# VectorE's seven-product work interleaved across row pairs, and more row pairs in that form, in a two-layer decoder trunk

## The chip, the cores and the metric

The kernel runs on one core of one Trainium2 chip. The metric is the device time of one execution in microseconds, from three runs given as a median with the lowest and the highest. TensorE (PE) multiplies, VectorE (DVE), ScalarE (ACT) and GpSimd (POOL) compute elementwise, and SyncE (SP) issues most of the weight transfers; each works through its own list of instructions in order and waits on semaphores for the others.

## What is computed

The reference is a trunk of two pre-norm layers on 256 tokens of width 2048, all in float32. Each layer has a token mixer beside a cross-attention into 256 memory tokens, an output projection, and a SwiGLU FFN of inner width 5632:

```python
for layer in range(DEPTH):                       # 2
    hn = _rmsnorm(h, norm_mix[layer])
    y, xq = _hgrn2_mixer(...) if layer == 0 else _gla_mixer(...)
    xa = _memory_attention(xq, mem_n, w_mem_kv[layer])
    h = h + jnp.concatenate([y, xa], axis=-1) @ w_out[layer]
    hn = _rmsnorm(h, norm_ffn[layer])
    gate, up = jnp.split(hn @ w_gate_up[layer], 2, axis=-1)
    h = h + (jax.nn.silu(gate) * up) @ w_down[layer]
return _rmsnorm(h, norm_final)
```

The two FFNs hold most of the work: a 2048 by 11264 product (gate and up together) and a 5632 by 2048 product each.

## The kernel before

**Float32 from three fast products.** A float32 factor is cut into a high part in the faster float32r type and a low part, the difference. One product of two tiles is three matmuls into one PSUM bank: high by high, high by low, low by high. For the weights `split` does the cutting (L276): ACT writes the high part (a CAST, or an ACTIVATE where the sign is turned), then DVE subtracts it from the raw weight and writes the low part (a TENSOR_TENSOR or SCALAR_TENSOR_TENSOR of 512 or 1024 columns). Twice in a block of the FFN POOL does the subtraction in DVE's place (`free_port`).

**Row pairs.** Weights come in row pairs: two blocks of 128 rows (the inner dimension), each with 512 columns of one kind (gate) and 512 of another (up), so that `raw` holds four 128x512 pieces. With the two token tiles of the activations this is a 2 by 2 product of blocks, and a pair has one of these kinds:

- **S**: seven products instead of eight (`seven`, L451), 21 matmuls. DVE must also form sums of weight pieces: `raw[:, 0]` becomes a difference (512 columns, called "less" here), then `raw[:, 2:4]` has it subtracted (1024 columns, "both less"). Four splits, named a (512 columns, of `raw[:, 0]`), b, c and d (1024 columns each): a and b before the sums, c and d of the sums. In the FFN the sum that c needs is put together by the transfer itself (`fed`): SP loads one row block into `raw[:, 1]`, then POOL issues an accumulating DMA of the other on top of it. For pairs 0 and 7 that sum lies in a tile of its own, T (`load_apart`).
- **O** and **H**: eight products, 24 matmuls. O needs two splits of 1024 columns on DVE and nothing else; H needs the same two, one difference of 512 columns and one split of 512 more. They use different sums of the activations, and `PAIRS` fixes for each pair which sums of activations are kept (`Forms`).
- In `project_two` (mixers, memory keys, output projection) the kinds are S and "-", a plain pair with eight products.

**The FFN.** `ffn` runs 11 blocks of 512 gate and 512 up columns (`up_block`). `project_halves` goes through the eight row pairs of a block with the kinds of `KINDS` (L1197): the fifth and later blocks all use its last entry, seven blocks in each layer. After each block come two "down" units of `project`, which multiply earlier results with `w_down` and accumulate onto `h` (`fd` in the trace); in the steady blocks these are four weight loads of 1024 KB. `sums` and `gate` turn the seven banks of a block (`f_p`) into the gated result, `turn` transposes it.

**What sets the order.** In the FFN the kernel's own order holds on each engine (`Engine.kept`). Small pieces of work (sums, gate, turn, `give_back`) are put off with `due` and come up at `mark(key + p)`, which `seven` calls between its splits b and c. `give_back` is two ACT copies of a down unit's PSUM banks to `h`; the steady blocks do it for their second unit inside pair 1 of the next block, ahead of split c of that pair. Buffers: `raw` has 3, `parts` (the 1024 column splits) 6, `part` (split a) 2; the pool waits for the last reader of a buffer before it is loaded or written again.

In the trace and in the order of the instructions the steady block that is looked at has the weight tiles 136 to 143 for row pairs 0 to 7 and 144 to 147 for its down units; `parts138c` is split c of pair 2, and `raw<-raw` are the two sums. The helper at L151 records nearly every operation of PE, DVE and ACT, so lines of code tell little there and tile names tell more.

## Time and profile before

| | |
|---|---|
| three runs | 2255.65 us median, 2253.49 to 2257.12 |
| the profiled execution | 2254.6 us, span of the core's instructions 2252.8 us |
| ACT busy | 1452.8 us, 64% of the span, 2010 instructions |
| POOL busy | 280.4 us, 12%, 275 instructions |
| PE weight loads busy | 1894.6 us, 84% (they overlap the matmuls) |
| mean granted TensorE clock | 0.999 of full speed |
| transfers | 477.28 MB, mean 212 GB/s |

Busy time is time in which an instruction of that engine ran; matmuls are pipelined and their ends are modelled, so that a busy PE tells that it was fed, and the spacing of its starts tells how fast. A timeline row has the start, the duration, the engine, the line, the operation, what is written and read, how many instructions were merged, and in brackets how long the engine stood idle before it and whose end it waited for. The fifth to eleventh blocks of an FFN are the steady ones: the fifth begins at 729.83 us in layer 0 and at 1773.06 us in layer 1, and the next ones follow every 61.45 to 61.69 us.

### The profile page before, as it was taken

What the parts mean: (1) busy time and instruction counts of PE and PEld (TensorE: products, weight loads), DVE (VectorE), ACT (ScalarE), POOL (GpSimd) and SP (SyncE); (2) the same over time, 40 slices, a digit from 0 to 9 for tenths busy, and PEclk for the clock granted to TensorE, in tenths of its full rate; (3) what the DMA queues carried; (4) which work ended last, traced back from release to release, by engine and by line L of the source; (5) the groups of instructions that cost most, each with busy time, mean ns of one, the idle gap of its engine ahead of it and who ended that gap; (6) DMA issues with size and microseconds to landing.
All of it is one profiled execution on the core that took longest, in us unless ns stands there. A gap on an engine that the chain in (4) does not pass through costs nothing.

```text
span 2252.8 us, 30400 instructions
## 1 busy us (share of the span) xinstructions
PE 2238.6 (99%) x10668; PEld 1894.6 (84%) x10668; DVE 2031.5 (90%) x2551; ACT 1452.8 (64%) x2010; POOL 280.4 (12%) x275
## 2 busy tenths in 40 slices
PE   9999999999999999999999999999999999999998
PEld 7888888888888888888889999988888888888887
DVE  6879899898998999999996887889999999999997
ACT  7656656565666666666665665566566676666664
POOL 1000100000111112112210000000011221212110
PEclk9999999999999999999999999999999999999999
DMA  8656655656687778878865445566677878887874
GB/s 296 215 168 213 199 182 177 200 193 190 198 236 232 229 234 231 230 230 238 244 221 168 141 156 182 164 209 197 208 221 224 233 230 238 242 238 236 231 233 167
DMA packets 255628, 477.28 MB, mean 212 GB/s; under 512 B 18255, under 2 KB 47731, under 8 KB 255219
## 3 DMA queue, kind: packets, MB, share of 16 engines
q1 hardware_dynamic: 228547, 420.21, 55.5%
q0 software_dynamic: 25632, 50.87, 13.0%
q10 hardware_dynamic: 1296, 4.26, 0.5%
q8 instruction: 84, 1.38, 0.2%
q14 instruction: 69, 0.57, 0.1%
HBM read 472.12 MB, written 3.15 MB: 211 GB/s over the span
## 4 chain that ended last, share of the span: by engine, by line
PE 90%; DVE 6%; issue 2%; DMA 1%; ACT 1%; SPq 0%; POOL 0%; DVEq 0%; POOLq 0%; ACTq 0%
PE f_p L151 34%; PE fd L151 18%; PE wo L151 4%; PE m1p L151 2%; PE hv2p L151 2%; PE hv1p L151 2%; PE hf0p L151 2%; PE hv0p L151 2%; PE wo1p L151 2%; PE hf2p L151 2%; PE hf1p L151 2%; PE wo0p L151 2%; PE m0p L151 2%; PE gk0p L151 1%; PE gk1p L151 1%
## 5 line engine op out<-in xcount | busy, mean ns | idle before, releaser
L151 DVE TENSOR_TENSOR raw<-raw 128x1024 f32<-128x1024 f32 (+3 forms) x330 | 311.2, 943 | 16.7 <-DMA raw<-in_w_down_dram 5.6
L151 ACT CAST parts<-raw 128x1024 fp32r<-128x1024 f32 (+1 forms) x216 | 211.7, 1016 | 56.8 <-DMA raw<-in_w_down_dram 14.7
L151 DVE TENSOR_TENSOR parts<-raw,parts 128x1024 fp32r<-128x1024 f32 (+1 forms) x176 | 200.2, 1171 | 22.7 <-ACT parts L151 22.0
L444 POOL DMA_DIRECT2D raw<-in_w_gate_up_dram x92 | 80.4, 873 | 541.2 <-DMA raw<-in_w_gate_up_dram 274.7
L300 POOL TENSOR_TENSOR parts<-raw,parts 128x1024 fp32r<-128x1024 f32 x40 | 95.6, 2406 | 113.5 <-ACT parts L151 81.2
L151 ACT COPY h<-fd 128x512 f32<-128x512 f32 x80 | 45.7, 588 | 46.5 <-PE fd L151 44.0
L428 POOL DMA_DIRECT2D T<-in_w_gate_up_dram x36 | 21.1, 587 | 430.2 <-DVE hf_4g L151 82.7
L151 ACT ACTIVATE s<-s,rf_r 128x512 f32<-128x512 f32 x44 | 31.8, 723 | 42.0 <-DVE s L151 42.0
L151 DVE SCALAR_TENSOR_TENSOR s<-e,rf_r,s 128x512 f32<-128x512 f32 x44 | 45.7, 1076 | 2.9 <-ACT s L151 0.5
L151 DVE TENSOR_TENSOR e<-f_p,e 128x512 f32<-128x512 f32 x66 | 45.2, 684 | 2.6 <-DVE s L151 0.5
L429 POOL DMA_DIRECT2D T<-in_w_gate_up_dram x36 | 31.0, 861 | 120.4 <-DMA T<-in_w_gate_up_dram 111.1
L151 ACT COPY fd<-h 128x512 f32<-128x512 f32 x82 | 45.2, 582 | 0.0
L444 POOL DMA_DIRECT2D raw<-in_hgrn_w_in_dram x17 | 14.7, 867 | 209.9 <-DMA raw<-in_hgrn_w_in_dram 124.6
L151 PE MATMUL fd<-parts,s_0h 128*128 128x512 f32 x128 | 39.8, 392 | 0.0
L151 PE MATMUL fd<-parts,s_4h 128*128 128x512 f32 x128 | 39.8, 392 | 0.0
L151 PE MATMUL fd<-parts,s_8h 128*128 128x512 f32 x128 | 39.8, 392 | 0.0
L151 PE MATMUL fd<-parts,s_2h 128*128 128x512 f32 x128 | 39.8, 392 | 0.0
L151 PE MATMUL fd<-parts,s_6h 128*128 128x512 f32 x128 | 39.8, 392 | 0.0
L151 PE MATMUL fd<-parts,s_1h 128*128 128x512 f32 x128 | 39.4, 389 | 0.0
L151 PE MATMUL fd<-parts,s_3h 128*128 128x512 f32 x128 | 39.4, 389 | 0.0
L151 PE MATMUL fd<-parts,s_5h 128*128 128x512 f32 x128 | 39.4, 389 | 0.0
L151 PE MATMUL fd<-parts,s_7h 128*128 128x512 f32 x128 | 39.4, 389 | 0.0
(6020 smaller groups left out, 7434.0 us busy)
## 6 DMA issues: line engine op xcount, KB each, us to landing
raw<-in_w_gate_up_dram SPq DMA_DIRECT2D x224, 512.0 KB, 4.4
raw<-in_w_down_dram SPq DMA_DIRECT2D x80, 1024.0 KB, 5.5
raw<-in_w_gate_up_dram SPq DMA_DIRECT2D x220, 256.0 KB, 4.2
raw<-in_hgrn_w_in_dram SPq DMA_DIRECT2D x79, 512.0 KB, 4.6
raw<-in_gla_w_in_dram SPq DMA_DIRECT2D x96, 384.0 KB, 3.3
raw<-in_w_gate_up_dram POOLq DMA_DIRECT2D x92, 256.0 KB, 4.9
T<-in_w_gate_up_dram POOLq DMA_DIRECT2D x72, 256.0 KB, 5.0
raw<-in_w_out_dram SPq DMA_DIRECT2D x16, 1024.0 KB, 5.1
```

The lines of the kernel that those rows point to most:

```text
L151: ins = func(*args, **kwargs)
L300: low = (nc.gpsimd if free_port else ve).tensor_tensor(out=both[:, 1, k:j, 0:m], in0=src[:, k:j, :], in1=both[:, 0, k:j, 0:m].bitcast(F32) ...
L428: nc.gpsimd.dma_start(out=both[:, 0, :], in_=rows[0])
L429: nc.gpsimd.dma_start(out=both[:, 0, :], in_=rows[1], accum_op=ALU.add)
L444: nc.gpsimd.dma_start(out=raw[:, 1, 0:n], in_=rows[1], accum_op=ALU.add)
```

## The change

Three things are changed.

1. **Interleaving.** `seven` gets an `ahead` call between its splits c and d: the tile of the next pair is taken, its loads are issued and its split a is done there, before split d of the present pair. "less" of a pair moves ahead of its split b, and "both less" comes after split b. With T apart, "both less" stands between the two halves of split c. In H pairs `ahead` comes before the small third split. `project_two` does the same where an S pair follows an S pair.
2. **More S pairs.** Row pair 5 keeps the activation sums of S (eight of them) in place of those of O (six). The fifth and later blocks of the FFN become `SSSSSSSS`, in the first four O becomes H at pair 5 (eight products as before). In the GLA mixer's key/query stages (`gk0`, `gk1`) there are two S pairs, not one.
3. **The order of the seven sums** of a block's banks in `sums`, and with it the two additions after which POOL takes a split.

```diff
-    def split(src, name, by=2, turned=False):
+    def split(src, name, by=2, turned=False, between=None):
...
+                if k:
+                    between()
...
-    PAIRS = "SSSSSOSB"
+    PAIRS = "SSSSSSSB"
...
-    def seven(i, raw, fed, between=None):
+    def seven(i, raw, fed, between=None, b00=None, ahead=None):
...
+        if not begun:
+            b00, = split(raw[:, 0:1, :], f"{i}a")
+        if not fed:
+            tt(out=raw[:, 1, :], in0=raw[:, 1, :], in1=raw[:, 2, :], op=ALU.add)
+        if fed and begun:
+            less()
         b11, b10 = split(raw[:, 2:4, :], f"{i}b")
         if between:
             between()
...
+        if not (fed and begun):
+            less()
+        if apart:
+            t6, t7 = split([raw[:, 0:1, :], apart], f"{i}c", turned=True, between=both_less)
+        else:
+            both_less()
+            t6, t7 = split(raw[:, 0:2, :], f"{i}c", turned=True)
+        if ahead:
+            ahead()
         t5, t4 = split(raw[:, 2:4, :], f"{i}d")
...
+        def ahead(p):
+            if p < len(PAIRS):
+                i, raw = come(p)
+                came.append((i, raw, split(raw[:, 0:1 if kinds[p] == "S" else 2, :], f"{i}a")))
...
-        project_two(hq["pairs"], ("------S-", "------S-")[pr], w, kw + pr * 2 * DK, pr * 2 * DK, 2 * DK, f"gk{pr}", give,
+        project_two(hq["pairs"], "-----SS-", w, kw + pr * 2 * DK, pr * 2 * DK, 2 * DK, f"gk{pr}", give,
...
-    KINDS = ("SHHSHOSO", "HHHSSOSO", "SHHSSOSO", "SSHSSOHS", "SSSSSOSS")
+    KINDS = ("SHHSHHSO", "HHHSSHSO", "SHHSSHSO", "SSHSSHHS", "SSSSSSSS")
...
-                for out, p, q in ((s0, 2, e0), (e1, 6, e0), (s1, 7, e1), (e1, 5, e1), (e0, 5, s1),
+                for out, p, q in ((e1, 6, e0), (s0, 2, e0), (s1, 7, e1), (e0, 5, s1), (e1, 5, e1),
                                   (s1, 4, s1), (e1, 3, e1)):
                     ve.tensor_tensor(out=out, in0=ps[p], in1=q, op=ALU.add)
-                    if p in (2, 5) and out is not e0 and b:
+                    if (p == 6 or out is e0) and b:
```

On DVE, in a steady block of layer 0, pair 2 (tile 138) and the start of pair 3 (139) stood so before; `raw_6651` is the tile of pair 2:

```order
L151 TENSOR_TENSOR parts138a<-raw_6651,parts138a 128x512
L151 TENSOR_TENSOR parts138b<-raw_6651,parts138b 128x1024
L151 TENSOR_TENSOR raw_6651<-raw_6651 128x512
L151 TENSOR_TENSOR raw_6651<-raw_6651 128x1024
L151 SCALAR_TENSOR_TENSOR parts138c<-raw_6651,parts138c 128x1024
L151 TENSOR_TENSOR parts138d<-raw_6651,parts138d 128x1024
L151 TENSOR_TENSOR parts139a<-raw_6691,parts139a 128x512
```

The same place on DVE now, from split a of pair 2 on; `raw_6652` is the tile of pair 2:

```order
L151 TENSOR_TENSOR parts138a<-raw_6652,parts138a 128x512
L151 TENSOR_TENSOR parts137d<-raw_6599,parts137d 128x1024
L151 TENSOR_TENSOR raw_6652<-raw_6652 128x512
L151 TENSOR_TENSOR parts138b<-raw_6652,parts138b 128x1024
L151 TENSOR_TENSOR raw_6652<-raw_6652 128x1024
L151 SCALAR_TENSOR_TENSOR parts138c<-raw_6652,parts138c 128x1024
L151 TENSOR_TENSOR parts139a<-raw_6692,parts139a 128x512
L151 TENSOR_TENSOR parts138d<-raw_6652,parts138d 128x1024
```

The six instructions of a pair are the same; split a of the next pair stands ahead of split d, and split b stands between the two sums, right ahead of the one that overwrites what it reads.

On DVE at pair 5 (tile 141), which was an O pair, and its neighbours, before:

```order
L151 TENSOR_TENSOR parts140d<-raw_6731,parts140d 128x1024
L151 TENSOR_TENSOR parts141a<-raw_6774,parts141a 128x1024
L151 TENSOR_TENSOR parts141b<-raw_6774,parts141b 128x1024
L151 TENSOR_TENSOR parts142a<-raw_6807,parts142a 128x512
L151 TENSOR_TENSOR parts142b<-raw_6807,parts142b 128x1024
```

The same place on DVE now:

```order
L151 TENSOR_TENSOR parts141a<-raw_6775,parts141a 128x512
L151 TENSOR_TENSOR parts140d<-raw_6732,parts140d 128x1024
L151 TENSOR_TENSOR raw_6775<-raw_6775 128x512
L151 TENSOR_TENSOR parts141b<-raw_6775,parts141b 128x1024
L151 TENSOR_TENSOR raw_6775<-raw_6775 128x1024
L151 SCALAR_TENSOR_TENSOR parts141c<-raw_6775,parts141c 128x1024
L151 TENSOR_TENSOR parts142a<-raw_6815,parts142a 128x512
L151 TENSOR_TENSOR parts141d<-raw_6775,parts141d 128x1024
```

Pair 5 has six instructions on DVE where it had two.

On ACT, at the start of that block, now; `h<-fd` are the two copies of `give_back`, `s_4h` belongs to `turn`:

```order
L151 CAST parts137b<-raw_6599 128x1024
L151 ACTIVATE s_4h<-tp_s_4h_6547 128x512
L151 ACTIVATE s_4h<-tp_s_4h_6552 128x512
L151 COPY h<-fd_1_3_0_0_6501 128x512
L151 COPY h<-fd_1_3_0_1_6502 128x512
L151 ACTIVATE parts137c<-raw_6599 128x1024
L151 CAST parts138a<-raw_6652 128x512
L151 CAST parts137d<-raw_6599 128x1024
```

Before, the first six of these rows stood in the same order; behind split c of pair 1 the cast of 137d came ahead of that of 138a, and now the two have changed places.

More of the change, by code (lines that the diff above doesn't have):

```diff
@@ L591, in early, with come @@
                 out[:] = onto
-        for at, (p, kind) in enumerate(zip(order, plan)):
+        came = []
+        def come(at):
             i, raw = new_raw()
             if i == 0:
-                load_pair(raw, w, p, c0, c1, n, kind, fed)
+                load_pair(raw, w, order[at], c0, c1, n, plan[at], fed)
             if prep:
@@ L599, in project_two, with ahead @@
             if i > 0:
-                load_pair(raw, w, p, c0, c1, n, kind, fed)
+                load_pair(raw, w, order[at], c0, c1, n, plan[at], fed)
+            return i, raw
+        def ahead(at):
+            i, raw = come(at)
+            came.append((i, raw, split(raw[:, 0:1, 0:n], f"{i}a")[0]))
+        for at, (p, kind) in enumerate(zip(order, plan)):
+            i, raw, b00 = came.pop() if came else (*come(at), None)
             if kind == "S":
-                todo = held(behind, seven, i, raw[:, :, 0:n], fed) if behind else seven(i, raw[:, :, 0:n], fed)
+                more = (lambda: ahead(at + 1)) if plan[at + 1:at + 2] == "S" else None
+                args = seven, i, raw[:, :, 0:n], fed, None, b00, more
+                todo = held(behind, *args) if behind else args[0](*args[1:])
                 last = at == plan.rindex("S")
@@ L638, in product, with come @@
             pe.matmul(ps[b], xl, hi, start=False, stop=left[b] == 0)
-        for p, kind in enumerate(kinds):
-            Engine.kept = keep <= p
+        came = []
+        def come(p):
             i, raw = new_raw()
@@ L644, in project_halves @@
                 apart[7] = load_apart(w, 7, c1)
-            fed = apart.get(p, True)
-            load_pair(raw, w, p, c0, c1, 512, kind, fed)
+            load_pair(raw, w, p, c0, c1, 512, kinds[p], apart.get(p, True))
+            return i, raw
+        def ahead(p):
+            if p < len(PAIRS):
+                i, raw = come(p)
+                came.append((i, raw, split(raw[:, 0:1 if kinds[p] == "S" else 2, :], f"{i}a")))
+        for p, kind in enumerate(kinds):
+            Engine.kept = keep <= p
+            i, raw, begun = came.pop() if came else (*come(p), None)
             x = forms[p].get
@@ L649, in project_halves @@
             if kind == "S":
-                todo = seven(i, raw, fed, lambda: mark(key + p))
+                todo = seven(i, raw, apart.get(p, True), lambda: mark(key + p), begun and begun[0], lambda: ahead(p + 1))
                 for b in (1, 2, 6, 7, 5, 4, 3) if last else (1, 3, 2, 6, 7, 5, 4):
@@ L653, in project_halves @@
             else:
-                b00, b01 = split(raw[:, 0:2, :], f"{i}a")
+                b00, b01 = begun or split(raw[:, 0:2, :], f"{i}a")
                 mark(key + p)
```

14 lines of the change are left out of this document (7 added, 7 removed).

## The prediction

> **What bounds the kernel now.** I read the page first, then the chain that ended last, then one steady block of the FFN engine by engine. The page's busy times:
>
> ```profile
> PE 2238.6 (99%) x10668; PEld 1894.6 (84%) x10668; DVE 2031.5 (90%) x2551; ACT 1452.8 (64%) x2010; POOL 280.4 (12%) x275
> ```
>
> PE is fed all the time, and VectorE has a tenth to spare on average. The average hides the stages, so next comes the chain, at one steady block (start, length, what):
>
> ```profile
> 791.29 38.81 PE f_p L151 x171
> 830.11 16.32 PE fd L151 x72
> 847.30 5.46 PE fd L151 x24
> 852.76 38.81 PE f_p L151 x171
> ```
>
> A block is a stretch of 171 f_p matmuls in 38.81 us, 227 ns each without a gap, then the down units; the next block begins 61.47 us later. By the stretches of time, VectorE is nearly full here:
>
> ```profile
> 791.29:852.76 61.47, 61.47 (x277) 50.94 (x276) 58.73 (x64) 41.74 (x54) 11.97 (x11) 1.00 0.79 227
> ```
>
> 58.73 of 61.47 us. So PE sets the time, and the fourteen steady blocks (seven in each layer) have VectorE close behind. How close is read from the timelines. ScalarE first:
>
> ```profile
> 790.71 1.27 ACT L151 COPY h<-fd 128x512 f32<-128x512 f32 x2 [2.31 <-PE fd L151]
> 791.87 1.06 ACT L151 ACTIVATE parts137c<-raw 128x1024 fp32r<-128x1024 f32 x1
> ...
> 825.40 1.06 ACT L151 CAST parts143d<-raw 128x1024 fp32r<-128x1024 f32 x1 [0.70 <-DVE raw L151]
> ```
>
> The two copies `h<-fd` wait for the last down matmul of the block before, that is, for the moment in which PE begins the new stretch (791.13 us, called t0). Split c of pair 1 (137c) stands behind them on ScalarE. VectorE:
>
> ```profile
> 792.96 1.23 DVE L151 SCALAR_TENSOR_TENSOR parts137c<-raw,parts137c 128x1024 fp32r<-128x1024 f32 x1 [0.96 <-ACT parts137c L151]
> 794.11 1.22 DVE L151 TENSOR_TENSOR parts137d<-raw,parts137d 128x1024 fp32r<-128x1024 f32 x1
> 795.24 0.68 DVE L151 TENSOR_TENSOR parts138a<-raw,parts138a 128x512 fp32r<-128x512 f32 x1
> 795.84 1.22 DVE L151 TENSOR_TENSOR parts138b<-raw,parts138b 128x1024 fp32r<-128x1024 f32 x1
> 796.98 1.94 DVE L151 TENSOR_TENSOR raw<-raw 128x512 f32<-128x512 f32 x2
> ...
> 813.31 1.22 DVE L151 TENSOR_TENSOR parts141a<-raw,parts141a 128x1024 fp32r<-128x1024 f32 x1
> 814.44 1.22 DVE L151 TENSOR_TENSOR parts141b<-raw,parts141b 128x1024 fp32r<-128x1024 f32 x1
> 815.58 0.69 DVE L151 TENSOR_TENSOR parts142a<-raw,parts142a 128x512 fp32r<-128x512 f32 x1
> ...
> 823.34 0.69 DVE L151 TENSOR_TENSOR raw<-T,raw 128x512 f32<-128x512 f32 x1
> 824.06 1.23 DVE L151 TENSOR_TENSOR raw<-raw 128x1024 f32<-128x1024 f32 x1
> 825.21 0.68 DVE L151 SCALAR_TENSOR_TENSOR parts143c<-T,parts143c 128x512 fp32r<-128x512 f32 x1
> 825.81 0.68 DVE L151 SCALAR_TENSOR_TENSOR parts143c<-raw,parts143c 128x512 fp32r<-128x512 f32 x1
> 826.49 1.22 DVE L151 TENSOR_TENSOR parts143d<-raw,parts143d 128x1024 fp32r<-128x1024 f32 x1
> ...
> 830.50 0.68 DVE L151 TENSOR_TENSOR e<-f_p,e 128x512 f32<-128x512 f32 x1
> 831.29 0.69 DVE L151 TENSOR_TENSOR s<-f_p,e 128x512 f32<-128x512 f32 x1
> ...
> 854.43 1.23 DVE L151 SCALAR_TENSOR_TENSOR parts149c<-raw,parts149c 128x1024 fp32r<-128x1024 f32 x1 [0.80 <-ACT parts149c L151]
> ```
>
> VectorE waited 0.96 us for 137c (0.80 for 149c, the same split a block later), so its place in each block is tied to PE: 137c begins at t0 + 1.83. From there to 143d it runs without a wait (its starts follow one another), 33.53 us. PE at the end of the stretch:
>
> ```profile
> 827.90 0.62 PE L151 MATMUL f_p<-parts143d,hf_7h 128*128 128x512 f32 x2
> 829.94 0.62 PE L151 MATMUL fd<-parts,s_3h 128*128 128x512 f32 x2
> ```
>
> The second of the two matmuls on 143d needs the low part that VectorE writes. It starts at 827.90 + 0.23 = 828.13; VectorE had it at 826.49 + 1.22 = 827.71. **The reserve is 0.42 us.** PE takes 21 x 0.227 = 4.76 us for an S pair, VectorE 6.03 (it goes from 795.24 at 138a to 813.31 at 141a, three pairs, in 18.07); it loses ground in each S pair, wins it back in the O pair (2.27 us on VectorE, 5.44 on PE), and arrives with nothing left. In the down units it cannot run ahead, because the next 137c waits for PE again.
>
> **The change part by part.** *PE.* Seven products in place of eight at pair 5 take away 3 matmuls in each of 14 blocks: 14 x 3 x 0.227 = 9.5 us. In the key/query stages it is 3 matmuls of 384 columns, twice:
>
> ```profile
> 1261.60 14.04 PE gk0p L151 x81
> ```
>
> 14.04 / 81 = 173 ns, so 6 x 0.173 = 1.0 us; VectorE has room there. If PE alone counted, that would be 10.6 us less.
>
> *VectorE's spacing.* Two 1024-column operations that don't depend on each other start 1.14 us apart (137d to 138a, 138b to the sum behind it), behind a SCALAR_TENSOR_TENSOR 1.15, and behind a 512-column one 0.60 (138a to 138b). One that waits for the one right ahead starts later: 0.72 instead of 0.60 (823.34 to 824.06). The two sums of a pair were such neighbours, and the interleaving parts them. But now "both less" stands right behind split b, whose source it overwrites. An H pair of an earlier block shows that case:
>
> ```profile
> 672.90 1.22 DVE L151 TENSOR_TENSOR parts114b<-raw,parts114b 128x1024 fp32r<-128x1024 f32 x1
> 674.15 0.69 DVE L151 TENSOR_TENSOR raw<-raw 128x512 f32<-128x512 f32 x1
> ```
>
> 1.25 us instead of 1.14. So a pair takes, from "less" on, 0.60 + 1.25 (b) + 1.14 (both less) + 1.15 (c) + 0.60 (next a) + 1.14 (d) = **5.88 us**, 0.15 less than before. If no wait were held there it would be 5.77, if every neighbour still cost what it did, 6.03; I take 5.88, since the H pair is the same two kinds of operations in the same relation. ScalarE's casts lie beside this: each of 1.06 us has over 2 us between what it needs and who needs it.
>
> The Trainium skill ("VectorE: DVE Perf Modes", section "The DRAIN you can't avoid") says against such a change that the pipeline flush comes after every VectorE operation and cannot be skipped by leaving out semaphores. By that rule the pair would stay at 6.03 us and the sum below would be 14 x 5 x 0.15 = 10.5 us longer; the 0.60 beside the 0.72 in the rows above disagrees.
>
> *VectorE's new path.* 137c still starts at t0 + 1.83: the copies stand ahead of it as before. Then 1.15 + 0.60 + 1.14 = 2.89 to the "less" of pair 2; pairs 2 to 6, five S pairs where there were four and an O, 5 x 5.88 = 29.40; pair 7: less 0.60, b 1.14, the T half of c 0.60, then "both less". Split d needs ScalarE's cast of that sum, which took 1.23 + 0.11 + 1.06 + 0.03 = 2.43 us from the start of the sum to the start of 143d (824.06 to 826.49). Before, both halves of c lay in that time, now only one, so it is a wait and stays 2.43. Sum 2.89 + 29.40 + 4.77 = 37.06; 143d starts at t0 + 38.89, where it was at 35.36. Its low part is there at 40.11, and from there PE took 829.94 - 828.13 = 1.81 us to the end of the stretch. **The stretch ends at t0 + 41.92 instead of 38.81: 3.11 us later per block**, the missing matmuls included, since PE now waits. 14 x 3.11 = 43.5 us. The down units take PE 61.47 - 38.81 = 22.66 us as before. VectorE has 22.66 + 1.83 + 41.92 - 38.89 = 27.52 us from 143d to the next 137c; it needed 27.14 (826.49 to the next one's 854.43, less 0.80 of waiting), so this holds, with 0.4 us in reserve; the new order of the sums parts two of four held neighbours there (830.50 to 831.29, 0.79 instead of 0.60), another 0.4.
>
> *Transfers.* The next load of a raw buffer starts when split d has read it, and "less" three pairs on needs that load and POOL's accumulation on top. For that there were 13.8 us (two pairs and a and b); now there are 3 x 5.88 less the 5.96 from "less" to the end of the pair's split d, 11.68. The chain, twice (SyncE's first load, POOL's accumulation), and the landing times of POOL's transfers in two windows:
>
> ```profile
> 795.35 0.33 SPq L443 DMA_DIRECT2D raw<-in_w_gate_up_dram  x1
> ...
> 918.28 0.33 SPq L443 DMA_DIRECT2D raw<-in_w_gate_up_dram  x1
> ...
> 800.62 0.86 POOL L444 DMA_DIRECT2D raw<-in_w_gate_up_dram  x1 [7.04 <-DVE parts138c L151]
> ...
> 924.36 0.86 POOL L444 DMA_DIRECT2D raw<-in_w_gate_up_dram  x1 [7.41 <-DVE parts162d L151]
> ```
>
> ```profile
> raw<-in_w_gate_up_dram POOLq DMA_DIRECT2D x2, 256.0 KB, 4.8
> ...
> raw<-in_w_gate_up_dram POOLq DMA_DIRECT2D x3, 256.0 KB, 6.3
> ```
>
> So 5.27 + 4.8 = 10.1 us up to 6.08 + 6.3 = 12.4. At the lower end nothing waits; at the upper end three pairs take 0.72 us more, 0.24 each, 1.2 in five. POOL has one accumulation more per block (pair 5), which stands between those of pairs 4 and 6 and delays them no more than that. I take 0.4 us per block, a third of the upper end, 5.6 us in all; with as much again where the 0.4 us in the down units is used up, the bound is 2.4 per block, 33.6 us.
>
> *O to H in the first four blocks.* Eight products as before. VectorE gets 1.2 us more per block (two operations of 512 columns), ScalarE 0.6. What hides it, in the fourth block:
>
> ```profile
> 667.05 40.12 PE f_p L151 x177
> ```
>
> ```profile
> 700.86 1.22 DVE L151 TENSOR_TENSOR parts119d<-raw,parts119d 128x1024 fp32r<-128x1024 f32 x1
> ```
>
> The last low part is there at 702.08, and PE needs it at 667.05 + 40.12 - 1.81 = 705.36. Nothing is counted. The only f_p wait for VectorE in the whole trace is one of 0.3 us in the second block of layer 0:
>
> ```profile
> PE f_p L151 <- DVE parts96c L151: 0.3, 1, 0.3
> ```
>
> There the cover is thin; without it 1 us per block, 2 at most in all. The larger activation sums of pair 5 and the interleaving in the mixers are counted at nothing: PE is full there. The span holds 2252.8 - 2238.6 = 14.2 us in which PE is idle, mostly at its ends; 5 us is the most that I allow to be won.
>
> **Sum:** 2254.6 (the profiled execution, 1.8 over its span and 1.0 below the median of the runs) + 43.5 + 5.6 - 1.0 = **2302.7 us**.
>
> **The rivals.**
> 1. *Faster: PE stays the bound.* For it: PE is at 99%, VectorE at 90%. Then the time is 2254.6 - 10.6 = 2244.0. It decides at 143d: it would have to start by 38.13 - 1.81 - 1.22 = 35.10 after t0, a path of 33.27 us instead of 37.06, so pairs of 5.12 us. Only if the copies didn't tie 137c to PE could that be. 0.06.
> 2. *Throughput: VectorE's idle time takes it up.* 58.73 + 3.53 of work, less 0.4 by the sums, is 61.86 us per block; were the waits free to move, a block would take that instead of 61.47: 14 x 0.39 - 1.0 = 4.5 more, 2259.1, just within no change. Against it stands the wait of 0.96 us, which is for PE and comes back in every block. 0.05. The Trainium skill ("Perfetto Trace Analysis", section "Identifying the Most-Contended Engine") calls VectorE's occupancy a fair measure of how close it is to its limit; by that this rival would hold, and the row that names the wait speaks against it.
> 3. *The same path with another spacing:* nothing held behind b, pairs of 5.77 us, 2.56 us per block: 2254.6 + 35.8 - 1.0 = 2289, 0.12. Or every neighbour costs what it did, pairs of 6.03: 2302.7 + 10.5 = 2313, 0.03; the 0.60 beside 0.72 speaks against that.
> 4. *The accumulated loads set the pair's time:* up to 2.4 us more per block, 2316 to 2332. 0.24.
>
> **How the numbers follow.** The forecast has 0.50. Faster by over 0.2% (about what a measurement of this kernel can tell from no change) is rival 1, 0.06; within 0.2% rival 2, 0.05; slower 0.89. The range covers the forecast and rivals 3 and 4: from 2289 less 5 us won elsewhere, 2284, to 2254.6 + 43.5 + 33.6 = 2332.
>
> **What would show it.** In the profile after: an f_p stretch of about 41.9 us for 168 matmuls and blocks 64.6 us or more apart; 137c still some 1.8 us after PE's first matmul; pairs 5.88 us apart on VectorE; PE waiting for VectorE's `parts` of pairs 5 to 7, longest at pair 7; in the second block of the FFN no more than a us. Wrong is the path if f_p stays gapless; wrong is the term for transfers if "less" waits for POOL's loads by more than 1 us per block.

## Result and the profile after

| | before | after |
|---|---|---|
| median of the runs, us | 2254.57 (four, 2252.85 to 2257.12) | 2311.47 (four, 2311.03 to 2317.22) |
| ratio | | 1.0257, interval 1.0242 to 1.0272 |
| span of the profiled execution | 2252.8 | 2309.0 |
| steady block, start to start | 61.47 | 64.70 |

The change makes the kernel 56.9 us slower, with 48 matmuls fewer. The page of the changed kernel, busy times and the chain that ended last:

```profile
PE 2259.4 (98%) x10620; PEld 1879.1 (81%) x10620; DVE 2089.5 (90%) x2637; ACT 1482.1 (64%) x2050; POOL 296.6 (13%) x289
...
PE 51%; DVE 21%; issue 12%; DMA 3%; ACT 2%; POOL 0%; SPq 0%; ACTq 0%; POOLq 0%; DVEq 0%
```

PE's share of the chain has fallen from about 90% to 51%; VectorE has 21% of it and "issue" 12%. (PE is called busy for longer although it does less, since the page counts a part of a matmul's wait as busy: in e12_one_more below a start comes 0.77 us behind the one before it where 0.23 is usual, and its row tells 0.39 us of idle time.) One steady block in the stretches of time (length; busy time of PE, weight loads, VectorE, ScalarE and POOL, each with its count; clock, share of the DMA engines, GB/s):

```profile
799.92:864.62 64.70, 62.59 (x274) 49.91 (x272) 61.59 (x68) 43.48 (x56) 12.80 (x12) 1.00 0.80 228
```

3.23 us more than the block before the change had. t0, PE's first matmul of the block, is at 799.92. First ScalarE's timeline there, then VectorE's:

```profile
799.49 1.27 ACT L151 COPY h<-fd 128x512 f32<-128x512 f32 x2 [2.27 <-PE fd L151]
800.65 1.06 ACT L151 ACTIVATE parts137c<-raw 128x1024 fp32r<-128x1024 f32 x1
```

```profile
801.75 1.23 DVE L151 SCALAR_TENSOR_TENSOR parts137c<-raw,parts137c 128x1024 fp32r<-128x1024 f32 x1 [0.95 <-ACT parts137c L151]
...
804.63 0.68 DVE L151 TENSOR_TENSOR raw<-raw 128x512 f32<-128x512 f32 x1
805.23 1.22 DVE L151 TENSOR_TENSOR parts138b<-raw,parts138b 128x1024 fp32r<-128x1024 f32 x1
806.48 1.23 DVE L151 TENSOR_TENSOR raw<-raw 128x1024 f32<-128x1024 f32 x1
...
810.50 0.68 DVE L151 TENSOR_TENSOR raw<-raw 128x512 f32<-128x512 f32 x1
...
837.46 0.69 DVE L151 SCALAR_TENSOR_TENSOR parts143c<-raw,parts143c 128x512 fp32r<-128x512 f32 x1
838.73 1.23 DVE L151 TENSOR_TENSOR parts143d<-raw,parts143d 128x1024 fp32r<-128x1024 f32 x1 [0.59 <-ACT parts143d L151]
```

137c waits 0.95 us for ScalarE, which had waited for PE's last down matmul, and starts at t0 + 1.83, as before. A pair takes 5.87 us (804.63 to 810.50); `both less` stands 1.25 us behind split b. 143d starts at t0 + 38.81 after a wait of 0.59 us for its cast. PE at the end of the stretch, and PE's waits in this block (total, times, longest):

```profile
838.20 0.50 PE L151 MATMUL f_p<-parts143c,hf_7h 128*128 128x512 f32 x1 [1.06 <-DVE parts143c L151]
...
840.01 0.50 PE L151 MATMUL f_p<-parts143d,hf_7h 128*128 128x512 f32 x1 [0.16 <-DVE parts143d L151]
...
841.96 0.62 PE L151 MATMUL fd<-parts,s_3h 128*128 128x512 f32 x2
```

```profile
PE f_p L151 <- DVE parts143c L151: 1.1, 1, 1.1
PE f_p L151 <- DVE parts142c L151: 0.4, 1, 0.4
PE f_p L151 <- DVE parts141c L151: 0.3, 1, 0.3
PE f_p L151 <- DVE parts143d L151: 0.2, 1, 0.2
```

PE now waits at pairs 5 to 7, longest at pair 7, and the stretch ends at t0 + 42.04. All fourteen steady blocks read like this one, and the twelve that another one follows take 64.69 to 64.71 us.

The 56.2 us between the two spans, from the first f_p matmul of each block: 14 x 3.23 = 45.2 in the steady blocks; 4.2 and 5.8 in the first four blocks of the two layers; 1.2 less between the FFNs; 1.35 more ahead of the first FFN, and about 1 at the end. So two things are to be explained: the 3.23 us, most of which were foreseen, and the 10 us of the early blocks, which were not.

### The profile page after: what moved, and what is told of

The parts are those of the page before. It is cut to its first block, busy times and chain, and to the rows that moved or that the text cites. A ratio compares the mean times of both kernels' runs of the same rounds, so it can differ in the third digit from the quotient of the medians.

```text
span 2309.0 us, 30544 instructions
## 1 busy us (share of the span) xinstructions
PE 2259.4 (98%) x10620; PEld 1879.1 (81%) x10620; DVE 2089.5 (90%) x2637; ACT 1482.1 (64%) x2050; POOL 296.6 (13%) x289
## 4 chain that ended last, share of the span: by engine, by line
PE 51%; DVE 21%; issue 12%; DMA 3%; ACT 2%; POOL 0%; SPq 0%; ACTq 0%; POOLq 0%; DVEq 0%
PE fd L151 15%; PE f_p L151 10%; DVE raw L151 4%; PE wo L151 4%; DMA raw<-in_w_gate_up_dram 2%; PE hv2p L151 2%; PE wo1p L151 2%; PE hf2p L151 2%; PE wo0p L151 2%; PE hv1p L151 1%; PE gg11p L151 1%; PE gg01p L151 1%; PE gg10p L151 1%; PE gk1p L151 1%; PE gg00p L151 1%
## 5 line engine op out<-in xcount | busy, mean ns | idle before, releaser
L151 DVE TENSOR_TENSOR raw<-raw 128x1024 f32<-128x1024 f32 (+3 forms) x372 | 347.5, 934 | 24.6 <-DMA raw<-in_w_gate_up_dram 9.9
L446 POOL DMA_DIRECT2D raw<-in_w_gate_up_dram x106 | 92.1, 869 | 563.9 <-DMA raw<-in_w_gate_up_dram 197.2
L151 DVE SCALAR_TENSOR_TENSOR s<-e,rf_r,s 128x512 f32<-128x512 f32 x44 | 57.8, 1353 | 2.5
```

The source lines that it names most:

```text
L151: ins = func(*args, **kwargs)
L446: nc.gpsimd.dma_start(out=raw[:, 1, 0:n], in_=rows[1], accum_op=ALU.add)
```

## The experiments

Each kernel ran beside the kernel before on one chip. The table has the time from one block's first f_p matmul to the next one's, in layer 0 (the first two blocks are one stretch, since no down units stand between them), and the steady blocks of layer 0 as a mean (layer 1 has the same to 0.07 us, but for e4_copies with 64.49). The first two blocks scatter by 0.6 us from trace to trace (97.30 to 97.90 in before, e12_one_more and e13_two_more, whose code is the same there); the third and the fourth agree to 0.01 us in these three. Kernels of one family stand together.

| kernel | blocks 1 and 2 | block 3 | block 4 | steady | time, us | ratio to before (interval) |
|---|---|---|---|---|---|---|
| before | 97.56 | 52.57 | 62.77 | 61.47 | 2254.6 | |
| after | 99.16 | 53.89 | 64.06 | 64.70 | 2311.5 | 1.0257 (1.0242 to 1.0272) |
| e2_kinds | 100.74 | 53.67 | 63.51 | 65.13 | 2316.3 | 1.0269 (1.0254 to 1.0285) |
| e12_one_more | 97.90 | 52.58 | 62.77 | 62.11 | 2263.3 | 1.0034 (1.0022 to 1.0047) |
| e13_two_more | 97.30 | 52.57 | 62.78 | 62.84 | 2274.1 | 1.0083 (1.0068 to 1.0098) |
| e3_h_at_5 | 98.56 | 55.64 | 64.05 | 63.27 | 2293.2 | 1.0167 (1.0152 to 1.0183) |
| e4_copies | 99.43 | 54.20 | 64.06 | 64.19 | 2307.4 | 1.0228 (1.0213 to 1.0243) |
| e10_after_s_to_s | 100.36 | 53.49 | 64.17 | 64.76 | 2313.4 | 1.0259 (1.0244 to 1.0274) |
| e1_interleave | 98.20 | 53.89 | 64.05 | 61.88 | 2270.1 | 1.0069 (1.0052 to 1.0086) |
| e6_third_in_parts | 96.72 | 53.93 | 62.77 | 61.88 | 2263.7 | 1.0040 (1.0026 to 1.0054) |
| e7_ahead_into_s | 96.71 | 52.95 | 63.15 | 61.44 | 2257.4 | 1.0013 (1.0004 to 1.0022) |
| e9_best | 97.85 | 52.95 | 63.14 | 61.44 | 2259.4 | 1.0025 (1.0015 to 1.0035) |
| e11_block4 | 97.37 | 52.94 | 62.76 | 61.47 | 2261.5 | 1.0027 (1.0016 to 1.0039) |
| e14_gk_sums | 96.98 | 52.58 | 62.77 | 61.46 | 2255.3 | 0.9998 (0.9989 to 1.0007) |

### One half of the change each: e1_interleave and e2_kinds

e1_interleave is the changed kernel with the old kinds (the edit below), e2_kinds the kernel before, its order of the sums too, with the new kinds:

```diff
-    PAIRS = "SSSSSSSB"
+    PAIRS = "SSSSSOSB"
-    KINDS = ("SHHSHHSO", "HHHSSHSO", "SHHSSHSO", "SSHSSHHS", "SSSSSSSS")
+    KINDS = ("SHHSHOSO", "HHHSSOSO", "SHHSSOSO", "SSHSSOHS", "SSSSSOSS")
-        project_two(hq["pairs"], "-----SS-", w, kw + pr * 2 * DK, ...
+        project_two(hq["pairs"], ("------S-", "------S-")[pr], w, kw + pr * 2 * DK, ...
```

> The interleaving and the new order of the sums alone; the kinds of the row pairs are those of before (O at pair 5, one S pair in the key/query stages). Theory (VectorE's path from 137c to 143d sets the steady blocks, and it grew by the S pair at pair 5): with the O pair back the path is at most 33.5 us, four pairs of 5.88 instead of 6.03, so PE is the bound again, f_p stretches of 38.8 us without a gap and steady blocks 61.4 to 61.5 us apart. For the first four blocks of each FFN, which cost some 10 us that the prediction didn't have: if the interleaving (split a of the next pair ahead of the small third split of an H pair, 'both less' held behind split b) is the cause, the 10 us stay and the time is about 2264 us; if O to H is the cause, they go and the time is about 2254.5 us. Rival to the theory (a neighbour costs what it did, the interleaving itself slows VectorE): steady blocks above 62 us.

> The kinds alone: S at pair 5 in the steady blocks, H for O in the first four, two S pairs in the key/query stages, all in the order of before, without interleaving. Theory: the path from 137c to 143d is that of before, 33.53 us, less 2.27 for the O pair and 6.03 more for an S pair, 37.29; 143d at t0 + 39.1, the stretch ends at t0 + 42.15, blocks 64.8 us apart, 3.34 more than before, so that the interleaving was worth only 0.1 us per block: 2254.6 + 46.8 - 1.0 = 2300 us if the 10 us of the first four blocks come from the interleaving, 2310 if they come from O to H. Rival (the interleaving itself is what costs, by its held neighbours): blocks at 62 us or less and a time below 2265 us.

**The kinds carry the loss of the steady blocks**: with them alone 65.13 us, without them 61.88. In e2_kinds VectorE's last part of 143c and PE's matmul that needs it:

```profile
838.97 0.68 DVE L151 SCALAR_TENSOR_TENSOR parts143c<-raw,parts143c 128x512 fp32r<-128x512 f32 x1
```

```profile
839.70 0.50 PE L151 MATMUL f_p<-parts143c,hf_7h 128*128 128x512 f32 x1 [1.29 <-DVE parts143c L151]
```

838.97 + 0.68 = 839.65, and PE goes on at 839.70. The expectation had 3.34 us per block, the trace has 3.66; what the 0.3 us are is settled by the next pair of runs. In these all-S blocks the interleaving, with the new order of the sums, was worth 65.13 - 64.70 = 0.43 us.

**The interleaving alone is not free either.** e1_interleave is 0.7% slower than before. Its steady blocks lose 0.41 us at one place, the S pair ahead of the O pair, on VectorE and on PE:

```profile
815.75 1.22 DVE L151 SCALAR_TENSOR_TENSOR parts140c<-raw,parts140c 128x1024 fp32r<-128x1024 f32 x1
816.88 1.22 DVE L151 TENSOR_TENSOR parts141a<-raw,parts141a 128x1024 fp32r<-128x1024 f32 x1
818.02 1.22 DVE L151 TENSOR_TENSOR parts140d<-raw,parts140d 128x1024 fp32r<-128x1024 f32 x1
```

```profile
819.29 0.50 PE L151 MATMUL f_p<-parts140d,hf_4h 128*128 128x512 f32 x1 [0.17 <-DVE parts140d L151]
```

Split a of the O pair (141a, 1024 columns, 1.14 us) now stands ahead of 140d, which PE needs at once. 141a is ready at 818.10, and PE takes its low part only at 820.78 by PE's timeline. The third and the fourth block lose as much as in the changed kernel (53.89 and 64.05 us, with O in place of H), so there the interleaving is enough; the first two lose less (98.20 for 99.16).

### How much reserve VectorE's path had: e12_one_more and e13_two_more

```diff
         b11, b10 = split(raw[:, 2:4, :], f"{i}b")
+        for _ in range(again):     # 1 or 2, pair 6 of the steady blocks
+            tt(out=b00[1], in0=raw[:, 0, :], in1=b00[0].bitcast(F32), op=ALU.subtract)
```

> The kernel before, with one more operation of 512 columns on VectorE in pair 6 of each steady block: the low part of split a is written a second time, with the same value, ahead of the difference. It adds 0.60 to 0.72 us to the path from 137c to 143d. Theory (the reserve at 143d is 0.42 us, at 143c 0.28): blocks 0.2 to 0.4 us longer, 61.7 to 61.9 us, the time 2254.5 + 3 to 6 = 2257 to 2260 us. Rival (throughput: VectorE's idle time of 2.7 us in a block takes it up): blocks of 61.47 and 2254.5 us.

> The same with two more operations of 512 columns in pair 6 of each steady block, 1.20 to 1.44 us. Theory: the second one costs its whole time, 0.60 to 0.72 us per block more than with one; blocks 0.8 to 1.1 us longer than before, 62.3 to 62.6 us, the time 2266 to 2270 us. Rival (throughput): blocks of 61.47 us still, since VectorE's work in a block is 58.73 + 1.3 = 60.0 us, and 2254.5 us.

VectorE has 2.7 us of idle time in a block of before, and one operation of 512 columns already costs 0.64 us, two cost 1.37. The idle time is no reserve, and both kernels come out above their forecasts (61.7 to 61.9 and 62.3 to 62.6 us). VectorE and PE in e12_one_more:

```profile
820.20 0.69 DVE L151 TENSOR_TENSOR parts142a<-raw,parts142a 128x512 fp32r<-128x512 f32 x1
820.92 1.95 DVE L151 TENSOR_TENSOR raw<-raw 128x512 f32<-128x512 f32 x2
...
829.41 0.68 DVE L151 SCALAR_TENSOR_TENSOR parts143c<-raw,parts143c 128x512 fp32r<-128x512 f32 x1
```

```profile
829.38 0.39 PE L151 MATMUL f_p<-parts143c,hf_7h 128*128 128x512 f32 x1
830.15 0.50 PE L151 MATMUL f_p<-parts143c,hf_7h 128*128 128x512 f32 x1 [0.39 <-DVE parts143c L151]
830.49 0.40 PE L151 MATMUL f_p<-parts143c,hf_7l 128*128 128x512 f32 x1
```

The added operation (142a a second time) takes 0.72 us (820.20 to 820.92). 143c is ready at 829.41 + 0.68 = 830.09, PE goes on at 830.15, 0.06 later; and the matmul after a wait takes 0.34 us to the next one (830.15 to 830.49) in place of 0.23. In the kernel before, 143c was ready at 825.81 + 0.68 = 826.49 (its row stands in the prediction). PE there:

```profile
826.54 0.62 PE L151 MATMUL f_p<-parts143c,hf_7h 128*128 128x512 f32 x2
```

The second of the two needs the low part and started at 826.54 + 0.23 = 826.77: a reserve of 0.28 - 0.06 = 0.22 us. So 0.72 - 0.22 + 0.11 = 0.61, measured 0.64, and 0.72 more for the second, measured 0.73. The same sum for e2_kinds: its path is 6.02 - 2.27 = 3.75 us longer, 3.75 - 0.22 + 0.11 = 3.64, measured 3.66. The reserve was **at 143c, not at 143d**.

### A pair with less for VectorE: e3_h_at_5

```diff
-    KINDS = (..., "SSSSSSSS")
+    KINDS = (..., "SSSSSHSS")
```

> The changed kernel with H in place of S at pair 5 of the steady blocks (eight products, 24 matmuls there). VectorE's part of the pair falls from 5.88 to about 3.6 us (1.14 for split a, 1.25 for split b held ahead of the difference, 0.60 for the difference, 0.60 for the third split), PE's rises from 4.76 to 5.44. Theory (pinned path): 143d starts at t0 + 36.5, its low part is there at 37.7, 0.7 us later than PE without a gap asks for it (37.0); stretches of 39.5 us for 171 matmuls, blocks 62.2 us apart, the time 2311.5 - 14 x 2.5 = 2276 us. Rival (VectorE's throughput decides, 61.6 - 2.3 = 59.3 us of work in a block): PE is the bound, blocks 61.5 us apart, 2266 us. Rival (the loads and POOL's accumulation decide): the pair loads the same bytes, blocks stay above 64 us.

63.27 us, neither of the two: the path theory had 62.2, throughput 61.5. 143d starts at t0 + 37.37 (block start 799.34) and not at 36.5. VectorE's timeline shows waits that the sum lacked:

```profile
824.91 0.69 DVE L151 TENSOR_TENSOR parts141c<-raw,parts141c 128x512 fp32r<-128x512 f32 x1 [0.17 <-ACT parts141c L151]
...
829.95 0.69 DVE L151 TENSOR_TENSOR parts143a<-raw,parts143a 128x512 fp32r<-128x512 f32 x1 [0.21 <-ACT parts143a L151]
...
830.90 1.22 DVE L151 TENSOR_TENSOR parts142d<-raw,parts142d 128x1024 fp32r<-128x1024 f32 x1 [0.26 <-ACT parts142d L151]
```

0.17 + 0.21 + 0.26 = 0.64 us of the 0.87 are waits for ScalarE's casts, which come close behind one another around the H pair. That throughput decides is out; this is the same block in the stretches of time (the columns as above):

```profile
799.34:862.59 63.25, 62.31 (x277) 50.72 (x275) 58.69 (x64) 42.28 (x55) 11.40 (x11) 1.00 0.78 225
```

VectorE has 58.69 us of work in 63.25, and PE still waits for it. That the loads decide is out too: the blocks are 1.4 us shorter with the same bytes.

### The tie to PE: e4_copies

```diff
-            dict(sums=10, gate=11, turn=((13, 101), (13, 101)), back=(13, 101)))
+            dict(sums=10, gate=11, turn=((13, 101), (13, 101)), back=(13, 101.5)))
...
         t5, t4 = split(raw[:, 2:4, :], f"{i}d")
+        if done:
+            done()                 # mark(key + p + 0.5)
```

> The changed kernel with ScalarE's two copies h<-fd of the steady blocks moved from ahead of split c of pair 1 to behind its split d; nothing else moves. Theory (the copies, which wait for PE's last down matmul, tie VectorE to PE): 137c no longer waits 0.95 us and starts about 1.0 us earlier after PE's first matmul; if nothing else ties VectorE there, blocks are 0.95 us shorter, 63.75 us, and the time is 2311.5 - 13 = 2298 us. Rival 1 (VectorE is simply short of time, the wait is made up elsewhere): blocks stay at 64.7 us, 2311 us. Rival 2 (throughput: all of VectorE's idle time can be used once the tie is gone): blocks near 61.9 us, 2272 us. If the copies now come too late for PE's bank, PE waits inside pair 0 and the blocks get longer.

The block that starts at 801.54, ScalarE and VectorE:

```profile
799.07 1.06 ACT L151 ACTIVATE parts137c<-raw 128x1024 fp32r<-128x1024 f32 x1 [0.30 <-PE fd L151]
802.47 0.62 ACT L151 CAST parts138a<-raw 128x512 fp32r<-128x512 f32 x1 [2.33 <-PE f_p L151]
802.99 1.05 ACT L151 CAST parts137d<-raw 128x1024 fp32r<-128x1024 f32 x1
803.95 1.06 ACT L151 COPY h<-fd 128x512 f32<-128x512 f32 x2
```

```profile
802.09 1.22 DVE L151 SCALAR_TENSOR_TENSOR parts137c<-raw,parts137c 128x1024 fp32r<-128x1024 f32 x1
```

137c now starts at t0 + 0.55, without a wait, and this block takes 63.83 us: 0.87 less than in the changed kernel, against 0.95 expected. **The copies were a tie that cost time.** But the next tie is at hand: the cast of 138a waits 2.33 us until PE has read split a of two pairs back (136a), whose buffer it takes. And in other blocks the load comes too late for the earlier start, here in the next one:

```profile
863.30 0.69 DVE L151 TENSOR_TENSOR raw<-raw 128x512 f32<-128x512 f32 x1 [1.36 <-DMA raw<-in_w_gate_up_dram]
```

That block takes 64.85 us, more than in the changed kernel. Over all, 4 us of the 13 were won.

### The early blocks: e6_third_in_parts, e7_ahead_into_s, e10_after_s_to_s

The third block of e1_interleave, ScalarE and VectorE, and behind them ScalarE in the kernel before:

```profile
624.20 0.62 ACT L151 CAST parts105a<-raw 128x512 fp32r<-128x512 f32 x1 [2.34 <-DMA raw<-in_w_gate_up_dram]
626.92 0.62 ACT L151 CAST parts104c<-raw 128x512 fp32r<-128x512 f32 x1 [2.09 <-PE f_p L151]
```

```profile
627.57 0.69 DVE L151 TENSOR_TENSOR parts104c<-raw,parts104c 128x512 fp32r<-128x512 f32 x1 [2.02 <-ACT parts104c L151]
```

```profile
623.10 0.62 ACT L151 CAST parts104c<-raw 128x512 fp32r<-128x512 f32 x1 [2.20 <-DVE raw L151]
624.76 0.62 ACT L151 CAST parts105a<-raw 128x512 fp32r<-128x512 f32 x1 [1.04 <-PE f_p L151]
```

The splits of 512 columns share two buffers (`part`). Before, they were written in the order 103c, 104c, 105a, and 105a had to wait for PE's last use of 103c. The interleaving makes it 103c, 105a, 104c: now 104c is the one that waits for PE, and with it all that stands behind it on ScalarE and VectorE.

The next wait of this kind follows, and in the third block it is the one that decides. The cast of 106a now stands ahead of that of 105d, and it must wait until PE has read 104c. e9_best, in which 104c is in its old place and doesn't wait for PE, shows it on ScalarE:

```profile
630.70 0.62 ACT L151 CAST parts106a<-raw 128x512 fp32r<-128x512 f32 x1 [0.91 <-PE f_p L151]
631.22 1.05 ACT L151 CAST parts105d<-raw 128x1024 fp32r<-128x1024 f32 x1
```

VectorE begins 106a at 16.53 to 16.54 us from the block's start in e1_interleave, in the changed kernel and in e9_best alike. So the wait of 104c costs the third block nothing by itself.

e6_third_in_parts (on e1_interleave) takes the third split out of these buffers; e7_ahead_into_s (also on e1_interleave) begins only S pairs ahead; e10_after_s_to_s is the changed kernel with `ahead` only from S into S:

```diff
 e6    -    e1, = split(raw[:, 3:4, :], f"{i}c")
       +    e1, = split(raw[:, 3:4, :], f"{i}c", ring=True)      # a buffer of `parts`
 e7    -    if p < len(PAIRS):
       +    if p < len(PAIRS) and kinds[p] == "S":
 e10   the line of e7, and in H pairs
       -    ahead(p + 1)
```

> Interleaving with the kinds of before (e1_interleave), and the small third split of an H pair written to a buffer of the six `parts` instead of one of the two `part`. Theory for the first four blocks: with `ahead`, split a of the next pair and the third split of an H pair share two `part` buffers in an order in which one of them has to wait until PE has read a split a or a third split that it needs much later (104c 2.0 us, 116a 1.7 us of VectorE's waiting on ScalarE, which waits for PE), so VectorE loses the lead that it had and split d of a later S pair comes 0.6 us late. With the other buffer these waits go, the third block falls from 53.89 to 52.6-52.9 us and the fourth from 64.05 to 62.8-63.2; the steady blocks have no H pair and stay at 61.88 (the stall at 140d is another cause); in all 2270 - 6 = 2264 us. Rival (the cause is the 1024-column split a of a following H or O pair, which stands 1.14 us ahead of split d): nothing changes, 2270 us.

> Interleaving with the kinds of before, but a pair is begun ahead only where it is an S pair; split a of an H or O pair (1024 columns) stays behind split d of the pair before. Theory (that split, 1.14 us ahead of split d, is what makes PE wait for 140d): the steady blocks fall from 61.88 to 61.47 us, 14 x 0.41 = 5.7 us; in the first four blocks split d of the S pair ahead of an O or H pair (87d, 96d, 106d, 116d) comes 1.14 us earlier, more than its 0.4 to 0.6 us of lateness, so most of their 7 us go too: 2270 - 5.7 - 6 = 2258 us. Rival (the buffers of the third split are the cause in the first four blocks): only the steady blocks get shorter, 2264 us.

> The changed kernel, all its kinds, but a pair is begun ahead only from an S pair into an S pair, as in e9_best. The steady blocks have S pairs alone and stay at 64.70 us. For the first four blocks, theory (two causes that overlap: the interleaving around H pairs delays VectorE by 1 to 2 us, and O to H gives it 1.2 us more work, which alone cost 9.5 us in e2_kinds without any interleaving): what is left is the work of O to H less what S pairs that follow S pairs gain, so some 5 to 8 of the 10 us stay, 2307 to 2310 us. Rival (O to H costs nothing once the interleaving is out of the H pairs): the first four blocks fall to those of e9_best, and the time to 2311.5 - 8 = 2303 us.

e6: the first two blocks and the fourth come back to 96.72 and 62.77 us, the kernel's time falls as expected (2263.7). The third block doesn't (53.93; 54.77 in layer 1). The waits of 104c and 106a for PE are gone there, but VectorE waits for a late load (4.46 us in layer 1):

```profile
623.23 0.68 DVE L151 TENSOR_TENSOR parts104c<-raw,parts104c 128x512 fp32r<-128x512 f32 x1
627.27 0.70 DVE L151 TENSOR_TENSOR raw<-raw 128x512 f32<-128x512 f32 x1 [3.35 <-DMA raw<-in_w_gate_up_dram]
```

e7: the steady blocks are back at 61.44 us, which shows that split a ahead of 140d was their whole loss, and the early blocks fall to 96.71, 52.95 and 63.15, within 0.4 us of before or below. So **both causes are real**: the buffers and the 1024-column split ahead of split d. In the fourth block either cure takes away most of the loss, so there it needed both; the steady blocks, without an H pair, had the second cause alone.

The 0.38 us that stay in the third and in the fourth block are the wait of 106a and of 116a, its like in the fourth block (e6, which is without it, has 62.77 there). VectorE and PE at 106c in the kernel before, and behind them VectorE in e9_best, which has the same 0.38 us:

```profile
635.32 1.22 DVE L151 SCALAR_TENSOR_TENSOR parts106c<-raw,parts106c 128x1024 fp32r<-128x1024 f32 x1
```

```profile
636.76 0.62 PE L151 MATMUL f_p<-parts106c,hf_4h 128*128 128x512 f32 x2
```

```profile
636.44 1.22 DVE L151 SCALAR_TENSOR_TENSOR parts106c<-raw,parts106c 128x1024 fp32r<-128x1024 f32 x1
```

Before, 106c was ready at 636.54, 22.22 us from the block's start, and PE took it at 636.76 + 0.23 = 636.99, a reserve of 0.45 - 0.06 = 0.39 us. In e9_best it is ready 22.85 us from the block's start, 0.63 later: 0.63 - 0.39 + 0.11 = 0.35, measured 0.38.

e10 misses its forecast: the early blocks lose 10.0 us as in the changed kernel, and the first two get worse (100.36). With H in place of O they lose time by another way, as in e2_kinds without any interleaving. PE's waits in e10 (e2_kinds has the same two):

```profile
PE f_p L151 <- DVE parts95c L151: 0.8, 1, 0.8
PE f_p L151 <- DVE parts98c L151: 0.8, 1, 0.8
```

The two losses don't add: kinds alone 9.6 us in the early blocks of both layers, interleaving alone 7.1, both 10.0.

### What can be kept: e9_best, e11_block4, e14_gk_sums

e9_best is e1_interleave with `ahead` only from S into S and two S pairs in the key/query stages. e11_block4 has `SSHSSOSS` in the fourth block besides. e14_gk_sums is the kernel before with the two S pairs and the new order of the sums, and nothing else.

```diff
 e9    -    project_two(hq["pairs"], ("------S-", "------S-")[pr], w, ...
       +    project_two(hq["pairs"], "-----SS-", w, ...
 e11   -    "SSHSSOHS"
       +    "SSHSSOSS"
```

> Interleaving only from an S pair into an S pair, none in H pairs, kinds of the FFN as before, but two S pairs in the key/query stages. Theory: every cost of the interleaving is taken out, PE is the bound everywhere as before, blocks of 61.47, and the key/query stages are worth 1.0 us: 2253.4 us, the same as before within what can be measured, a hair below. Rival (the interleaving or the order of the sums has another cost): 2258 us or more.

> The kernel e9_best with the kinds of the fourth block changed from SSHSSOHS to SSHSSOSS (three matmuls less in each layer, 1.4 us in all). Theory (VectorE's path): the fourth block has 3.3 us in reserve at 119d; an S pair in place of the H pair takes 5.9 instead of 3.6 us, 2.3 more, 1.0 stays, so PE stays the bound and the time is 1.4 us below e9_best, 2252 us. Rival (no reserve, since the buffers tie VectorE to PE): a fourth block of 63 us or more, no gain or a loss.

> The kernel before with the two parts of the change that don't touch VectorE's path in the FFN: two S pairs in the key/query stages and the new order of the sums; no interleaving, kinds of the FFN as before. Theory: PE stays the bound in every block (61.47 us), the six matmuls less are worth up to 1.0 us, 2253.5 us; the order of the sums nothing, since VectorE has that time in the down units. Rival (the larger sums of weights in the key/query stages need VectorE where it is late): up to 2 us more than before.

e9_best misses its forecast by 6 us. The 0.4 us stay in the third and in the fourth block of each layer, and the last FFN block's f_p stretch is 1.6 us longer in layer 0 and 0.9 in layer 1; the rest was not followed further. In layer 0 it is a late load (VectorE waits for a gate/up load once in the whole kernel before, 0.4 us):

```profile
1127.10 1.95 DVE L151 TENSOR_TENSOR raw<-raw 128x512 f32<-128x512 f32 x2 [1.59 <-DMA raw<-in_w_gate_up_dram]
```

e11_block4 gains 0.38 us in the fourth block of layer 0 where 0.68 were expected, but not in the whole time, 2261.5 against 2259.4; its trace is longer between the FFNs and behind the last block, where the code is that of e9_best. e14_gk_sums is the same as before within the measurement; between the FFNs its trace shows the 1.2 us that the changed kernel gains there too (421.55 us against 422.75). But e12_one_more and e13_two_more, with the code of before there, have 422.1 and 421.1, so this difference alone shows no gain. No version was faster than the kernel before.

## Why the prediction was right, and where it was off

- **The tied start and the path.** Right: 137c at t0 + 1.83 as forecast, 143d at t0 + 38.81 for 38.89, the end of the stretch at 42.04 for 41.92. e4_copies shows that the copies are the tie.
- **The spacing.** Right: 5.87 us for 5.88, so rival 3 is out. In e2_kinds, without interleaving, it is 6.02 (as is 18.07 / 3 in the kernel before; the prediction's 6.03 is a hundredth high). The pair has the same six operations in both traces, and only their order differs. The prediction took from the Trainium skill ("VectorE: DVE Perf Modes", section "The DRAIN you can't avoid") that the pair would stay at 6.03, but that section also says that a next operation which is not held starts earlier. The traces agree with that sentence as far as they go: independent neighbours start 0.60 and 1.14 us apart (512 and 1024 columns), dependent ones 0.72 and 1.25.
- **The reserve.** The step "the reserve is 0.42 us", taken at 143d, named the wrong place: it was tightest at 143c with 0.22 us, as e12_one_more and e13_two_more show. For the changed kernel it did little harm, since there the wait of 143d for its cast (0.59 us) makes 143d late as well, and PE waits for it last (840.01). From there PE took 1.95 us to the end of the stretch (841.96) and not 1.81: a matmul after a wait costs 0.11 us more, which the sum didn't have.
- **Transfers.** The mechanism is there, its size was too large in the steady blocks: 5.6 us were set down. VectorE does wait for gate/up loads in the changed kernel (total, times, longest):

```profile
DVE raw L151 <- DMA raw<-in_w_gate_up_dram: 9.9, 13, 2.1
```

But the steady blocks with such a wait are as long as those without (64.69 to 64.71 us): in pair 1 it ends before 137c's tie does, and nothing is lost. Rival 4 is out. In the early blocks of layer 1 such a wait may cost: behind the longest, 2.1 us, PE waits 0.6 us at 294d, which has no counterpart in layer 0, and these blocks lose 5.8 us where those of layer 0 lose 4.2. This was not tested. Where VectorE was made to come earlier, in e4_copies, e6_third_in_parts and e9_best, loads that came 1.4 to 4.5 us late were the next limit.
- **O to H in the first four blocks.** Here the prediction failed: nothing was counted, at most 2 us, and 10.0 were lost. Two steps were wrong. The cover was read at the end of the fourth block (3.3 us at 119d), and it was less in the middle of the blocks (0.39 us at 106c): PE now waits at the S pair ahead of an O or H pair (87d, 96d, 106d, 116d), and in e2_kinds and e10_after_s_to_s, with H in place of O and no interleaving there, at 95c and 98c. And the interleaving was counted only for the steady blocks; that `ahead` would change which split waits for PE's buffer, and would put 1024 columns ahead of split d, stands in the order of the instructions and was not followed into the blocks with H pairs.
- **Key/query stages.** Right: 1.0 us forecast. The two stretches that hold the six matmuls fall from 14.06 to 13.65 and from 24.38 to 23.86 us from first to last start on PE, 0.9 together. The 1.35 us ahead of the first FFN can't be put down to the change: e12_one_more and e14_gk_sums, whose code is that of before up to there, start their first FFN 1.9 and 1.6 us later than before.
- **Rivals 1 and 2.** Out. PE is not the bound with the new kinds. VectorE's idle time took up next to nothing: a block takes 64.70 us with 61.59 of work, and in the kernel before one added operation of 0.72 us made a block 0.64 longer. The Trainium skill ("Perfetto Trace Analysis", section "Identifying the Most-Contended Engine") takes occupancy for a fair measure of how close VectorE is to its roofline, the most that it can do; at 58.73 of 61.47 us the limit of this kernel was 0.22 us away, not 2.7.

The sum came out 8.8 us too low: 10.0 us of the early blocks were missing, the steady blocks with the transfers were 3.9 too high (49.1 for 45.2), and the rest lies ahead of the first FFN and at the end. That the total came this near is partly luck: the 5.6 us for transfers, which did not show in the steady blocks, stood in for more than half of what was missing in the early ones. The path alone, 43.5 us for 45.2, is no luck.

What stays open: why loads come 1.4 to 4.5 us late in some blocks and not in others (the third block of e3_h_at_5 has a wait of 2.8 us for one, that of the changed kernel, with the same order there, has none), and how the loss of H in place of O without interleaving spreads over the first two blocks. A third `part` buffer, which might take the waits of 104c, 106a and 138a away without moving them, was not tried.

## What to carry to other kernels

A spare tenth of an engine's time can be worth next to nothing if that engine is tied to another one at each round, as here: measure the path from the tie to the deadline, and look for the tightest deadline along it, not at the last one. When instructions are put earlier to fill gaps, ask for each what it now stands ahead of, and whose buffer it takes: a small operation that was free becomes a wait if the buffers are handed out in another order. Removing one tie won, here, only up to the next one.

## What the runs showed of the hardware

- In these traces a matmul of 512 columns that had to wait for its operand is followed 0.34 us later by the next one, not 0.23 (830.15 to 830.49 in e12_one_more); PE goes on 0.05 to 0.06 us after VectorE's write has ended (839.65 to 839.70 in e2_kinds, 830.09 to 830.15).
- VectorE's spacing depends on the neighbour: 1.25 us for two operations of 1024 columns where the second overwrites what the first reads (805.23 to 806.48), 1.13 to 1.15 where the two are independent and neither waits for another engine (816.88 to 818.02). The 0.72 us behind a 512-column operation, known from a sum that reads what the one ahead of it wrote, is also the price where the second overwrites what the first read (820.20 to 820.92).
